# Passages of the chunk scans: first inverse a tile sooner, loads spread, triangular products one by one, casts behind the last zi copy

## The chip, the cores and the metric

The kernel runs on one core of one Trainium2 chip. It is one launch on fp32 data: a whole encoder block with attention, a bidirectional RWKV-7 scan, gates, a squared-ReLU MLP and a gated input embedding. The metric is the device time of one execution in microseconds (us), lower is better. The engines are TensorE (PE, matmuls; PEld are its weight loads), VectorE (DVE), ScalarE (ACT), GpSimd (POOL) and SyncE (SP, which issues most loads).

## The reference, cut to what matters

```python
# x (1, 1024, 1024); 8 query heads, 2 key heads of 64; 8 RWKV heads of 64
proj = rms_norm(x, norm_mix) @ w_in
attn = windowed_gqa(q, k, v, sink)              # +-128 tokens
rw = rwkv7_time_mix(zr, ...)                    # forward and backward scan
gates = sigmoid(proj[..., O_GATE:])             # two branches of 1024 columns
merged = gates[0] * (attn @ w_up_attn) + gates[1] * (rw @ w_up_rwkv)
x = x + merged @ w_out
x = x + square(relu(rms_norm(x, norm_ffn) @ w_ff1)) @ w_ff2
x = x + (p @ w_ple) * sigmoid(rms_norm(x, norm_ple) @ w_ple_gate)

def step(state, inp):                           # the scan, one token
    sa = einsum('dbhij,dbhj->dbhi', state, a_t)
    state = state * w_t + sa * b_t + v_t * k_t
    y = einsum('dbhij,dbhj->dbhi', state, r_t)
```

The change touches the middle of this: attention, the scan, the gates and the lift of the attention by `w_up_attn`.

## The kernel before, in words

**Dense products.** Each fp32 operand is split into a high part (`split`, line 200: a cast on ACT to a shorter matmul type) and the rest (line 201: a subtraction on DVE). A product is three matmuls of parts (hi·hi, lo·hi, hi·lo). Weights arrive as `wst` (or `wust` for `w_up_attn`) and become `whi`/`wlo` (`wuhi`/`wulo`).

**Stages.** First the norm, the projection and the preparation of the RWKV operands, which go to DRAM as `ra_d`, `bk_d`, `v_d`. Then attention in eight tiles `n` of 128 queries. Each makes masked scores `smk` on DVE, transposes them (`pT`), multiplies with the values (`po`) and stores to `at_d`. The gates of the first 512 tokens (half 0) fill PE beside it at the lowest priority: `gates`, 16 products `gmm` over weights `wst`, a tanh `gth` on ACT, a store to `g_d`. `GQ` lists those gates whose weights are loaded by POOL's queue and not by SP's.

**The scan** runs in chunks of 64 tokens, 16 steps `s`, both directions at once, in blocks of four steps. A block needs the inverse of a triangular matrix per chunk and head. Its parts are: the triangular products `lps` of loads `la` and `lb` (`low_products`: per chunk 16 matmuls into two PSUM buffers, evicted by a pair of ACT copies `lt`); four ACT copies `Lc`; a transpose `Lp` and 31 steps of `tmp` and `Z` on DVE; two transposes `Zn` and `Zt`; and `inverse_off`, which makes `Q` and `zi` by small matmuls `qps` with copies (DVE four, ACT four, lines 881 and 882). The first block's products and inverse stand inside the attention, after the tiles that `LOW_AT` and `INV_AT` name. Those of the next blocks stand inside the steps 0, 4 and 8 (`aside(i)`, which calls `low`, and `inverse_steps`, whose DVE steps `inverse_turn` deals out), and `end_inverse` closes them at the end of each fourth step.

**One step** is, in program order: the carried part `wy`, the sum of `W`, the first products `gps` two steps ahead (evicted by DVE as `gm`, line 1187), `gap(0)`, `aside(0)`, `gap(1)`, `u_part` (`ups`, copied by ACT to `UV`; next `wa`, copied to `W`), the second products, `gap(2)`, `gap(3)`, `aside(1)`, `s_part` (`sps`, needs `UV`), `y_part`, `aside(2)`, `gap(4)`, in steps 0, 4 and 8 `aside(3)`, then `gap(5)`, `operands` (`tmps`), and two more gaps. A `gap` is a run of dense matmuls: the gates of half 1, and when these are done the lift of the attention (`uaps`, in `beside`, from `wuhi` and `aTh`). `gps`, `lps`, `qps` and `tmps` share two PSUM buffers.

**What sets the order.** Inside the scan PE's matmuls (`mmo`) and the DVE work marked `turn` stay in program order. Everything else (ACT's casts and copies, DVE's `wlo`, all loads) is placed by a static scheduler. Each engine then works through its list in order, and each DMA queue likewise. `after(x, y)` puts `x` behind `y`.

Of the kernel before, what the change touches and what calls it, by code (L numbers as in the profile page):

```python
# [55 lines left out]
GATT = 0  # L56
GQ = ((0, 1), (0, 2), (1, 0), (1, 1), (1, 2), (1, 3), (1, 4))
LOADS_AT = 6
# [10 lines left out]

LOW_AT = (2, 3)  # L70
INV_AT = 4
GN_EPS = 64e-5
# [75 lines left out]
def block_kernel(ctx: ExitStack, tc: tile.TileContext, I: dict, out: bass.AP):  # L148
# [46 lines left out]

    on_pool = [None]

    def split(hi, lo, src, lo_eng=None, pin=False, behind=None):

        a = nc.scalar.copy(hi, src)  # L200
        b = (lo_eng or nc.vector).tensor_tensor(out=lo, in0=src, in1=hi.bitcast(F32), op=ALU.subtract)  # L201
        for x_, y_ in zip((a, b), behind or ()):
            after(x_, y_)
        if lo_eng is nc.gpsimd:
            on_pool[0] = b
        if pin:
            tc.keep_in_program_order(a)
            tc.keep_in_program_order(b)
        return a, b
# [116 lines left out]
    def gates(h, ms=range(2 * KT), mm=nc.tensor.matmul, lo_of=lambda m: nc.gpsimd):  # L326

        for m in ms:
# [5 lines left out]
            nc.scalar.activation(out=th, in_=ps, func=AF.Tanh, scale=0.5)  # L334
            nc.sync.dma_start(g_d[m, :, 512 * h:512 * h + 512], th)
            yield
# [519 lines left out]
    def inverse_off(pl, ps_of, lt, zz, zi, mm, between):  # L856
# [23 lines left out]
        for k in range(2):  # L880
            nc.scalar.copy(zi[g[0], k::2, 32:64], qss[0][g[2 * k]])
            nc.scalar.copy(zi[g[3], k::2, 0:32], qss[1][g[3 - 2 * k]])

# [117 lines left out]
    sR, sU, sC, sRB = (ExitStack() for _ in range(4))  # L1001
    epi = {}
    def beside():
        def load_at(h):
            for k in range(NP):
                nc.sync.dma_start(epi["at"][k], at_d[:, k, 512 * h:512 * h + 512])

        def load_wu(pl, m):
            st = pl.tile([P, NP, P], F32, name="wust", tag="wu_st", bufs=2)
            nc.sync.dma_start(st, I["w_up_attn"][m])  # L1010
            return st

        yield from gates(1, range(GATT, LOADS_AT), mmo, lo_of=lambda m: nc.vector)
        load_at(0)
        sts = [load_wu(B, m) for m in range(2)]
        yield from gates(1, range(LOADS_AT, 2 * KT), mmo, lo_of=lambda m: nc.vector)
# [15 lines left out]
        def weights(m, st=None):  # L1032
            hi = UA.tile([P, NP, P], F32R, name="wuhi", tag="wu_hi", bufs=3)
            lo = UA.tile([P, NP, P], F32R, name="wulo", tag="wu_lo", bufs=3)
            split(hi, lo, load_wu(UA, m) if st is None else st)
            return hi, lo

        def part(k):
            split(aTh[:, k, :], aTl[:, k, :], epi["at"][k])

# [41 lines left out]
    def epilogue(e):  # L1082
# [17 lines left out]
        def parts2(p, src):  # L1100

            hi, lo = (r.rearrange("q p (a t) -> q p a t", a=2)[:, p] for r in (rwh, rwl))
            split(hi, lo, src)
            return hi, lo
# [231 lines left out]
    def begin_low(b):  # L1336
        lows[b] = low_products(BI, B, 3, ps_gps, b, mmo)
        next(lows[b])
# [10 lines left out]
    load_v(0)  # L1349
    begin_low(1)  # L1350
    for hf in range(2):
# [3 lines left out]
    fill(FILL0)  # L1355
    was = []

    def second_step():
# [13 lines left out]
    for s in range(NCH):  # L1372
# [4 lines left out]
        def gap(i):  # L1377

            fill(FILL[s % NB if s // NB < 3 else 1][i] if more else FILLEND)
# [17 lines left out]
        if nxt:  # L1397
            load_v(s + 1)
        gap(0)
        aside(0)  # L1400
        inverse_turn(TURNS[s % NB][0])
        gap(1)
        W = u_part(s, W)
        if more:
# [3 lines left out]
        gap(3)  # L1408
        aside(1)
        if nxt:  # L1410
            s_part(s)
        y_part(s)
        aside(2)
        gap(4)
        if s % NB == 0 and s // NB < 3:
            aside(3)
            inv[0] = inverse_steps(s // NB + 1)
# [610 lines left out]
```

## Time and profile before

| | |
|---|---|
| time, median of 3 runs | 1656.66 us (1656.21 to 1661.19) |
| the profiled execution | 1657.06 us, span 1655.2 us |
| PE busy | 1598.1 us (97%) |
| DVE / ACT / POOL busy | 1138.6 / 839.3 / 89.6 us |
| DMA | 269.23 MB, mean 163 GB/s |

A timeline row has the start, the duration, the engine, the line, output<-inputs, the shape and a count of instructions; in brackets stand the idle time of the engine just before and what ended it ("issue" is a wait for nothing that the profile shows). The attention runs here up to about 443 us after the span's start, the scan from about 450 to 800. In a table of stretches the fourth number from the end of a row is POOL's busy time with its count, the last three are the granted clock of PE, the DMA share and GB/s.

### The profile page before, as it was taken

The page shows a single profiled execution, that of the slowest core. Times are in us where ns is not written, and L with a number is a line of the kernel's source. Part 1 is how long each engine was busy: PE and PEld are TensorE (multiplying, and loading weights), DVE is VectorE, ACT ScalarE, POOL GpSimd, SP SyncE. Part 2 cuts the span into 40 slices and gives each one's busy share as a digit, 9 for nine tenths or more (in the row PEclk, how much of TensorE's full clock was granted, in tenths as well). Part 3 has the DMA queues.
Part 4 walks back from the last instruction along what each step waited for, and adds up shares of the span by engine and source line. Part 5 has one row for each costly group of instructions (what it writes and reads, how often), then busy time and mean ns, then how long its engine had stood idle before and what let it go on. Part 6 is the DMA issues. An engine that isn't in the chain of part 4 may idle for free.

```text
span 1655.2 us, 31169 instructions
## 1 busy us (share of the span) xinstructions
PE 1598.1 (97%) x12280; PEld 1295.4 (78%) x12280; DVE 1138.6 (69%) x2071; ACT 839.3 (51%) x1533; POOL 89.6 (5%) x111
## 2 busy tenths in 40 slices
PE   7999999999989999799999999999999999999998
PEld 6987777767668777676788778888888888888887
DVE  6648998477939678777826876766658877675332
ACT  5557888378553554555304554444445445444221
POOL 3440000210010000000000000000000000000000
PEclk9999999999999999899999999999999999999999
DMA  6362555855476644458722264444459855564010
GB/s 227 84 151 89 172 175 174 260 160 164 142 222 176 184 140 149 136 186 268 246 80 111 79 195 147 140 148 158 157 185 336 272 189 179 167 199 146 32 42 38
DMA packets 199938, 269.23 MB, mean 163 GB/s; under 512 B 47728, under 2 KB 103920, under 8 KB 199792
## 3 DMA queue, kind: packets, MB, share of 16 engines
q1 hardware_dynamic: 188736, 250.47, 47.5%
q0 software_dynamic: 10912, 16.26, 3.5%
q8 instruction: 96, 1.57, 0.4%
q10 hardware_dynamic: 144, 0.52, 0.1%
q14 instruction: 50, 0.41, 0.1%
HBM read 186.45 MB, written 80.74 MB: 161 GB/s over the span
## 4 chain that ended last, share of the span: by engine, by line
PE 72%; DMA 10%; DVE 7%; ACT 6%; issue 3%; POOL 1%; SPq 0%; ACTq 0%; DVEq 0%; POOLq 0%
PE ff1ps L1657 16%; PE ff2ps L1909 13%; PE gmm L226 5%; DMA wst<-in_w_col_dram 3%; PE mm L244 2%; PE mm L245 2%; PE mm L246 2%; PE plps L236 2%; PE plps L234 2%; PE plps L232 2%; PE gps L226 1%; PE mmo L245 1%; PE mmo L246 1%; PE wy L226 1%; PE mmo L244 1%
## 5 line engine op out<-in xcount | busy, mean ns | idle before, releaser
L1909 PE MATMUL ff2ps<-tl,sh 128*128 128x512 f32 x448 | 174.5, 390 | 0.2 <-DVE tl L201 0.2
L1909 PE MATMUL ff2ps<-th,sl 128*128 128x512 f32 x448 | 174.4, 389 | 0.0
L1909 PE MATMUL ff2ps<-th,sh 128*128 128x512 f32 x448 | 174.0, 389 | 0.0
L200 ACT CAST sh<-sst 128x512 fp32r<-128x512 f32 x109 | 67.8, 622 | 105.7 <-PE ff2ps L1909 50.8
L201 DVE TENSOR_TENSOR sl<-sst,sh 128x512 fp32r<-128x512 f32 x109 | 75.2, 690 | 47.6 <-ACT sh L200 47.2
L1657 PE MATMUL ff1ps<-mh,w1h 128*128 128x512 f32 x256 | 100.3, 392 | 2.0 <-ACT w1h L200 2.0
L200 ACT CAST whi<-wst 128x512 fp32r<-128x512 f32 x100 | 60.3, 618 | 78.7 <-DMA wst<-in_w_col_dram 39.3
L1657 PE MATMUL ff1ps<-ml,w1h 128*128 128x512 f32 x256 | 99.9, 390 | 0.0
L1657 PE MATMUL ff1ps<-mh,w1l 128*128 128x512 f32 x256 | 99.7, 390 | 0.0
L1909 PEld LDWEIGHTS ff2ps<-tl,sh 128*128 128x128 f32 x448 | 84.1, 188 | 18.4 <-DVE tl L201 0.8
L1909 PEld LDWEIGHTS ff2ps<-th,sh 128*128 128x128 f32 x448 | 84.0, 188 | 17.7 <-ACT th L200 0.3
L1909 PEld LDWEIGHTS ff2ps<-th,sl 128*128 128x128 f32 x448 | 84.1, 188 | 17.4
L200 ACT CAST w1h<-w1st 128x512 fp32r<-128x512 f32 x48 | 28.4, 620 | 106.7 <-DMA w1st<-in_w_ff_dram 66.5
L201 DVE TENSOR_TENSOR wlo<-wst,whi 128x512 fp32r<-128x512 f32 x88 | 58.9, 686 | 20.6 <-ACT whi L200 18.6
L185 POOL TENSOR_TENSOR rstd<-ms,neghalf 128x1 f32<-128x1 f32 x24 | 14.8, 615 | 1016.4 <-PE ff2ps L1909 573.1
L201 DVE TENSOR_TENSOR w1l<-w1st,w1h 128x512 fp32r<-128x512 f32 x48 | 31.8, 688 | 49.8 <-ACT w1h L200 49.8
L1657 PEld LDWEIGHTS ff1ps<-mh,w1h 128*128 128x128 f32 x256 | 48.0, 188 | 13.0 <-ACT w1h L200 2.9
L1657 PEld LDWEIGHTS ff1ps<-mh,w1l 128*128 128x128 f32 x256 | 48.1, 188 | 11.1 <-DVE w1l L201 1.0
L1657 PEld LDWEIGHTS ff1ps<-ml,w1h 128*128 128x128 f32 x256 | 48.1, 188 | 10.0
L232 PE MATMUL gmm<-hh,whi 128*128 128x512 f32 x128 | 52.2, 408 | 3.1 <-ACT whi L200 2.5
L1187 DVE TENSOR_TENSOR gm<-gps,gmask 128x384 f32<-128x384 f32 x64 | 32.6, 550 | 31.4 <-PE gps L226 31.2
L226 PE MATMUL gmm<-hl,whi 128*128 128x512 f32 x128 | 52.8, 413 | 1.0 <-issue 1.0
(406 smaller groups left out, 4503.8 us busy)
## 6 DMA issues: line engine op xcount, KB each, us to landing
tst<-in_w_ff_dram SPq DMA_DIRECT2D x80, 256.0 KB, 4.1
wst<-in_w_col_dram SPq DMA_DIRECT2D x78, 256.0 KB, 3.8
w1st<-in_w_ff_dram SPq DMA_DIRECT2D x32, 512.0 KB, 4.9
hid_S<-h SPq DMA_DIRECT2D x64, 256.0 KB, 2.1
sst<-hid_S SPq DMA_DIRECT2D x64, 256.0 KB, 3.4
hid_A<-h SPq DMA_DIRECT2D x48, 256.0 KB, 2.0
sst<-hid_A SPq DMA_DIRECT2D x45, 256.0 KB, 3.8
ra_d<-ra SPq DMA_DIRECT2D x8, 1024.0 KB, 6.1
```

Source lines behind the costliest of these rows:

```text
L200: a = nc.scalar.copy(hi, src)
L201: b = (lo_eng or nc.vector).tensor_tensor(out=lo, in0=src, in1=hi.bitcast(F32), op=ALU.subtract)
L226: tc.keep_in_program_order(nc.tensor.matmul(*a, **kw))
L232: mm(ps, ah, bh, start=(i == 0), stop=False)
L234: mm(ps, ah, bl, start=False, stop=False)
L236: mm(ps, al, bh, start=False, stop=(i == n - 1))
L244: nc.tensor.matmul(ps, ah, bh, start=(i == 0), stop=False)
L245: nc.tensor.matmul(ps, ah, bl, start=False, stop=False)
L246: nc.tensor.matmul(ps, al, bh, start=False, stop=(i == n - 1))
L1187: turn(nc.vector.tensor_tensor(out=gm[hf][:, s % NB, e].rearrange("p (a b) t -> p a b t", b=2), in0=pss[e][:, 0:6].rearrange("p (a b) t -> ...
L1657: nc.tensor.matmul(ps, x_[:, k, :], y_[:, k, :], start=start and k + i == 0, stop=k == 3 and i == 2, skip_group_check=True)
L1909: nc.tensor.matmul(banks[bs][i], x_[:, isl], y_, start=fresh and p + j == 0, stop=p == NPR - 1 and j == 2, skip_group_check=True)
```

## The change

It has six parts.

1. `LOW_AT` goes from (2, 3) to (1, 2) and `INV_AT` from 4 to 3: the first block's triangular products and its inverse stand one attention tile earlier.
2. `GQ` gains (0, 3): the weights of that gate are loaded by POOL's queue.
3. `begin_low(1)`, which issues the first loads `la` and `lb` of the second block, is called behind `operands(0)`.
4. The loads of `at_d` and of the first two `wust` are held behind the last gate store issued ahead of them (`epi["stored"]`).
5. In the steps 0, 4 and 8 the second triangular product stands between `gap(1)` and `u_part`, the third where the second was, and the fourth behind `y_part`, ahead of `gap(4)`. Before, the third and fourth stood around `gap(4)`.
6. The casts of `wuhi`, `aTh` and of the epilogue's `rwh` get `behind=(epi["zi"], None)`: ACT does them behind the last `zi` copy that has been recorded when they are written.

```diff
-GQ = ((0, 1), (0, 2), (1, 0), (1, 1), (1, 2), (1, 3), (1, 4))
+GQ = ((0, 1), (0, 2), (0, 3), (1, 0), (1, 1), (1, 2), (1, 3), (1, 4))
...
-LOW_AT = (2, 3)
-INV_AT = 4
+LOW_AT = (1, 2)
+INV_AT = 3
...
     def split(hi, lo, src, lo_eng=None, pin=False, behind=None):
...
         for x_, y_ in zip((a, b), behind or ()):
-            after(x_, y_)
+            if y_:
+                after(x_, y_)
...
-            nc.sync.dma_start(g_d[m, :, 512 * h:512 * h + 512], th)
+            epi["stored"] = nc.sync.dma_start(g_d[m, :, 512 * h:512 * h + 512], th)
...
-            nc.scalar.copy(zi[g[3], k::2, 0:32], qss[1][g[3 - 2 * k]])
+            epi["zi"] = nc.scalar.copy(zi[g[3], k::2, 0:32], qss[1][g[3 - 2 * k]])
...
-        def load_at(h):
+        def load_at(h, behind=None):
             for k in range(NP):
-                nc.sync.dma_start(epi["at"][k], at_d[:, k, 512 * h:512 * h + 512])
-
-        def load_wu(pl, m):
+                a = nc.sync.dma_start(epi["at"][k], at_d[:, k, 512 * h:512 * h + 512])
+                if behind:
+                    after(a, behind)
+
+        def load_wu(pl, m, behind=None):
             st = pl.tile([P, NP, P], F32, name="wust", tag="wu_st", bufs=2)
-            nc.sync.dma_start(st, I["w_up_attn"][m])
+            a = nc.sync.dma_start(st, I["w_up_attn"][m])
+            if behind:
+                after(a, behind)
             return st
...
-        load_at(0)
-        sts = [load_wu(B, m) for m in range(2)]
+        load_at(0, epi["stored"])
+        sts = [load_wu(B, m, epi["stored"]) for m in range(2)]
...
-            split(hi, lo, load_wu(UA, m) if st is None else st)
+            split(hi, lo, load_wu(UA, m) if st is None else st, behind=(epi["zi"], None))
...
-            split(aTh[:, k, :], aTl[:, k, :], epi["at"][k])
+            split(aTh[:, k, :], aTl[:, k, :], epi["at"][k], behind=(epi["zi"], None))
...
-            split(hi, lo, src)
+            split(hi, lo, src, behind=(epi["zi"], None))
...
     load_v(0)
-    begin_low(1)
     for hf in range(2):
         products(0, hf)
         fill(FILL0)
     operands(0)
     fill(FILL0)
     was = []
+    begin_low(1)
...
+        first = s % NB == 0 and s // NB < 3
         gap(0)
         aside(0)
         inverse_turn(TURNS[s % NB][0])
         gap(1)
+        if first:
+            aside(1)
         W = u_part(s, W)
...
-        aside(1)
+        aside(2 if first else 1)
         if nxt:
             s_part(s)
         y_part(s)
-        aside(2)
+        aside(3 if first else 2)
         gap(4)
-        if s % NB == 0 and s // NB < 3:
-            aside(3)
+        if first:
             inv[0] = inverse_steps(s // NB + 1)
```

A diff row tells little of the lists that come out. Here they are at three places. The first is DVE between the first inverse's end and the first products of the scan (`gm` is the eviction of `gps`, `wlo` belongs to the gates, `zi` are the four DVE copies). Before:

```order
L842 TENSOR_TENSOR Z<-Z,tmp 128x31
L849 STREAM_TRANSPOSE Zn<-Z 128x32x32
L850 STREAM_TRANSPOSE Zt<-Z 128x32x32
L871 COPY zi<-Zn 32x32x32
L1187 TENSOR_TENSOR gm_4576<-gps,gmask 128x384 x2
L871 COPY zi<-Zt 32x32x32 x2
L871 COPY zi<-Zn 32x32x32
L1187 TENSOR_TENSOR gm_4577<-gps,gmask 128x384 x2
L201 TENSOR_TENSOR wlo<-wst,whi 128x512 x2
```

and with the change:

```order
L844 TENSOR_TENSOR Z<-Z,tmp 128x31
L851 STREAM_TRANSPOSE Zn<-Z 128x32x32
L202 TENSOR_TENSOR wlo<-wst,whi 128x512 x2
L873 COPY zi<-Zn 32x32x32 x2
L852 STREAM_TRANSPOSE Zt<-Z 128x32x32
L873 COPY zi<-Zt 32x32x32 x2
L202 TENSOR_TENSOR wlo<-wst,whi 128x512 x2
L1192 TENSOR_TENSOR gm_4576<-gps,gmask 128x384 x2
L1192 TENSOR_TENSOR gm_4577<-gps,gmask 128x384 x2
```

Three `zi` copies and two pairs of `wlo` moved ahead of the first `gm`.

The second is ACT in step 4 (`lt` and `Lc` belong to the triangular products, `UV` and `W` to `u_part`, `whi` and `gth` to the gates, `tm` to `operands`). Before:

```order
L821 COPY lt<-lps 128x4x64 x2
L1304 COPY Lc<-lt 32x256 x4
L1256 COPY UV<-ups 64x512 x2
L1235 COPY W<-wa 128x512
L200 CAST whi<-wst 128x512 x2
L821 COPY lt<-lps 128x4x64 x2
L1304 COPY Lc<-lt 32x256 x4
L1284 COPY y<-wy_6132 128x2x2x64
```

and with the change:

```order
L823 COPY lt<-lps 128x4x64 x2
L1309 COPY Lc<-lt 32x256 x4
L823 COPY lt<-lps 128x4x64 x2
L1309 COPY Lc<-lt 32x256 x4
L1261 COPY UV<-ups 64x512 x2
L1240 COPY W<-wa 128x512
L201 CAST whi<-wst 128x512 x2
L823 COPY lt<-lps 128x4x64 x2
```

The second round of `lt` and `Lc` moved ahead of `UV` and `W`.

The third is ACT at the last closing of an inverse (end of step 11; `rwh` are casts for the epilogue, `wuhi` and `aTh` for the lift of the attention). Before:

```order
L868 COPY Q<-qps 32x16x32 x4
L334 ACTIVATE gth<-gmm 128x512
L200 CAST rwh_8667<-y 128x512 x4
L881 COPY zi<-qps 32x16x32
L882 COPY zi<-qps 32x16x32
L200 CAST wuhi<-wust 128x512
L200 CAST aTh<-gm_4576 128x512 x2
L200 CAST aTh<-gm_4577 128x512 x2
L200 CAST wuhi<-wust 128x512
L881 COPY zi<-qps 32x16x32
L882 COPY zi<-qps 32x16x32
```

and with the change:

```order
L870 COPY Q<-qps 32x16x32 x4
L336 ACTIVATE gth<-gmm 128x512
L883 COPY zi<-qps 32x16x32
L884 COPY zi<-qps 32x16x32
L883 COPY zi<-qps 32x16x32
L201 CAST wuhi<-wust 128x512
L201 CAST aTh<-gm_4576 128x512 x2
L201 CAST aTh<-gm_4577 128x512 x2
L201 CAST wuhi<-wust 128x512
L884 COPY zi<-qps 32x16x32
L201 CAST rwh_8667<-y 128x512 x3
```

The four `rwh` casts moved behind the last `zi` copy; two `wuhi` and four `aTh` still stand ahead of it.

More of the change, by code (lines that the diff above doesn't have):

```diff
@@ L196, in block_kernel @@
     on_pool = [None]
+    epi = {}
     def split(hi, lo, src, lo_eng=None, pin=False, behind=None):
@@ L1001, in block_kernel @@
     sR, sU, sC, sRB = (ExitStack() for _ in range(4))
-    epi = {}
     def beside():
-        def load_at(h):
+        def load_at(h, behind=None):
             for k in range(NP):
-                nc.sync.dma_start(epi["at"][k], at_d[:, k, 512 * h:512 * h + 512])
-        def load_wu(pl, m):
+                a = nc.sync.dma_start(epi["at"][k], at_d[:, k, 512 * h:512 * h + 512])
+                if behind:
+                    after(a, behind)
+        def load_wu(pl, m, behind=None):
             st = pl.tile([P, NP, P], F32, name="wust", tag="wu_st", bufs=2)
-            nc.sync.dma_start(st, I["w_up_attn"][m])
+            a = nc.sync.dma_start(st, I["w_up_attn"][m])
+            if behind:
+                after(a, behind)
             return st
         yield from gates(1, range(GATT, LOADS_AT), mmo, lo_of=lambda m: nc.vector)
-        load_at(0)
-        sts = [load_wu(B, m) for m in range(2)]
+        load_at(0, epi["stored"])
+        sts = [load_wu(B, m, epi["stored"]) for m in range(2)]
         yield from gates(1, range(LOADS_AT, 2 * KT), mmo, lo_of=lambda m: nc.vector)
```

## The prediction

> **What bounds the kernel now.** I read the page first, then the gaps of TensorE (PE) in the timeline, then a table of stretches for the granted clock, then the rows of VectorE (DVE) and ScalarE (ACT) around each gap.
>
> ```profile
> span 1655.2 us, 31169 instructions
> PE 1598.1 (97%) x12280; PEld 1295.4 (78%) x12280; DVE 1138.6 (69%) x2071; ACT 839.3 (51%) x1533; POOL 89.6 (5%) x111
> PE 72%; DMA 10%; DVE 7%; ACT 6%; issue 3%; POOL 1%; SPq 0%; ACTq 0%; DVEq 0%; POOLq 0%
> ```
>
> PE is busy for 97% of the span and carries 72% of the chain that ended last. The change adds no matmul and takes none away, so it can only win where PE stands idle or runs at half clock. The whole of PE's idle time is 1655.2 − 1598.1 = 57.1 us. These are its gaps in the stretch that the change touches (start, duration, work, then the idle time ahead and what ended it):
>
> ```profile
> 454.91 2.01 PE L226 MATMUL gps<-rac,bkc 64*64 64x128 f32 x32 [2.97 <-DVE gm L1187]
> ...
> 466.78 0.62 PE L226 MATMUL wa<-UV,gm 64*64 64x64 f32 x15 [2.00 <-issue]
> ...
> 478.24 0.39 PE L226 MATMUL gmm<-hl,whi 128*128 128x512 f32 x1 [1.01 <-issue]
> ...
> 492.30 1.10 PE L1204 MATMUL tmps<-ident,bkc 128*128 128x128 f32 x5 [0.81 <-ACT lt L821]
> ...
> 545.09 1.01 PE L226 MATMUL gps<-rac,bkc 64*64 64x128 f32 x32 [0.94 <-PE wy L226]
> ...
> 559.15 1.09 PE L1204 MATMUL tmps<-ident,bkc 128*128 128x128 f32 x8 [0.80 <-ACT lt L821]
> ...
> 676.70 0.79 PE L226 MATMUL wy<-rac,Sc 64*64 64x64 f32 x25 [1.34 <-issue]
> 681.39 2.14 PE L226 MATMUL gps<-rac,bkc 64*64 64x128 f32 x32 [3.06 <-ACT zi L881]
> ```
>
> Each part of the change aims at one of these: the first `gm` eviction (2.97), the wait after it (2.00), the triangular products in each fourth step (0.81, 0.80), and the last `zi` copies (3.06). Beside the gaps stands the clock. The next rows are stretches of 3.41 us (and three longer ones): length, then busy time and instructions of PE, weight loads, DVE, ACT and POOL, then granted clock, DMA share and GB/s.
>
> ```profile
> 451.63:455.04 3.41, 0.44 (x4) 0.13 (x4) 3.35 (x5) 0.21 (x2) 0.00 (x0) 1.00 1.14 276
> 455.04:458.45 3.41, 3.41 (x36) 2.75 (x36) 3.35 (x7) 1.11 (x2) 0.00 (x0) 0.50 1.27 214
> 460.00:480.00 20.00, 15.48 (x446) 11.52 (x445) 4.36 (x8) 7.44 (x14) 1.47 (x3) 1.00 0.77 237
> ...
> 489.18:492.59 3.41, 2.13 (x38) 1.33 (x38) 1.29 (x2) 3.31 (x11) 2.19 (x4) 1.00 0.91 221
> 492.59:496.00 3.41, 3.41 (x24) 2.56 (x26) 1.37 (x1) 3.04 (x7) 0.00 (x0) 0.50 0.98 333
> ...
> 680.32:683.74 3.42, 2.35 (x33) 1.99 (x34) 3.24 (x7) 2.19 (x4) 0.00 (x0) 0.50 0.89 282
> 404.00:454.30 50.30, 47.27 (x271) 33.42 (x267) 47.43 (x151) 31.76 (x86) 2.69 (x5) 1.00 0.42 133
> ```
>
> After the 2.97 us gap PE runs 3.41 us at clock 0.50, after which the clock is 1.00 again. Such a passage does half of its work and so costs 3.41 / 2 = 1.7 us. The gap of 2.00 us at 464.78 is followed by none (460 to 480 has 1.00 throughout).
>
> **Part 1: the first inverse one attention tile sooner (LOW_AT, INV_AT).** It neither adds nor removes work; it moves the first block's products and its 31 DVE steps. Here is DVE ahead of the first `gm`, and PE's gate products beside it:
>
> ```profile
> 439.86 0.42 DVE L965 COPY pT<-pt 128x256 f32<-128x256 f32 x1
> ...
> 449.65 2.15 DVE L849 STREAM_TRANSPOSE Zn<-Z 128x1024 f32<-128x1024 f32 x1
> 451.67 1.89 DVE L850 STREAM_TRANSPOSE Zt<-Z 128x1024 f32<-128x1024 f32 x1
> 453.58 0.68 DVE L871 COPY zi<-Zn 32x1024 f32<-32x1024 f32 x1
> 454.30 1.02 DVE L1187 TENSOR_TENSOR gm<-gps,gmask 128x384 f32<-128x384 f32 x2
> ...
> 458.28 1.28 DVE L201 TENSOR_TENSOR wlo<-wst,whi 128x512 fp32r<-128x512 f32 x2
> ```
>
> The first `gm` starts 454.30 − 440.28 = 14.0 us after the last transposed tile of the attention (439.86 + 0.42 = 440.28, the common zero below). The second `gps` product needs its buffer and waits for it. With the change the chain starts one tile sooner: two stores of `at_d` stand at
>
> ```profile
> 419.31 0.53 SPq L974 DMA_DIRECT2D at_d<-at  x1
> 432.87 0.52 SPq L974 DMA_DIRECT2D at_d<-at  x1
> ```
>
> that is 13.56 us apart. But DVE then has three more things to do between the chain's start and the first `gm`. One is an attention tile, which in these groups (busy us, mean ns) is
>
> ```profile
> L943 DVE CUSTOM_DVE_ANT_0 smk<-sc,band 128x256 f32<-128x256 f32 (+1 forms) x8 | 3.5, 451 | 0.2
> L965 DVE COPY pT<-pt 128x384 f32<-128x384 f32 (+1 forms) x5 | 2.5, 527 | 0.2
> L960 DVE TENSOR_SCALAR smk<-smk,es 128x384 f32<-128x384 f32 (+1 forms) x4 | 1.4, 382 | 0.0
> ```
>
> with small ones of about 1.6 beside it: 9.0. The others are, by the order of the changed kernel, four `wlo` (two pairs of 1.28, 2.55) and three `zi` copies (3 × 0.68 = 2.05) that stood behind the first `gm`. That is 13.6 more work for 13.56 us more time. What gains is DVE's idle time: 50.30 − 47.43 = 2.87 us of the stretch 404 to 454 in which it waited, and which the earlier start lets it use. I take 2.2 of it, so the first `gm` starts at +11.8 and its first half is done at +12.4. PE arrives sooner too: the order shows 25 gate matmuls in place of 30 between the attention's last product and the first `gps`, each 0.235 us start to start, so PE wants the second `gps` not at 451.94 − 440.28 = +11.66 but at +10.45. The wait is then 12.4 − 10.45 = 1.95 instead of 2.97, worth 1.0. A wait of 2.00 stands in the quoted rows without half clock, so the 1.7 us of the passage go too: **−2.7**. Bounds: −4.7 (no wait: 2.97 + 1.7), and +0.1, because DVE takes its work in order and the second pair of `wlo` now stands ahead of `gm`. That pair needs its weights, which come on the POOL queue while the DMA share is 1.14 to 1.27: if they land late, `gm` is late, and the stall is as before. The value is nearer the middle because the wait only has to fall under about 2 us.
>
> The Trainium skill ("TensorE: Matmul & The Clock Gate", section "What's actually happening") says that the clock falls to half after an idle window of some 3.4 us, in windows of 3413 ns that run free. The trace agrees on the length of a passage (3.41) and on the window at 451.63, which is nearly idle (0.44 busy). It does not agree at 492.59, where the window before was busy for 2.13.
>
> **Part 2: loads spread.** Half of these eight loads (issues of one line, their ns, first and last start) and two `wust` loads, 1.5 MB in all, move on SP's queue:
>
> ```profile
> L1006 SPq DMA_DIRECT2D gm<-at_d x8: 382/428/659, 472.8 to 681.4; - x8
> ```
>
> from 472.8 to behind the store of gate 5's results, which SP issues near 540. There they stand ahead of two `rac` and two weight loads that have a step to arrive in. They lie under matmuls in both places: the issue wait near the old place is 1.01 (478.24), near the new one 0.94 (545.09, without the burst), so I take 0, with +1.0 if the burst brings a wait to the new place and leaves none saved at the old one. Opening the second block's products moves behind `operands(0)`; its first two pairs of loads keep their place in SP's order, the third now stands behind a gate store. That thins the traffic around 464, where PE waits 2.00 for "issue", twice the other issue waits (1.01, 0.94, 1.34). I take it down to theirs: **−1.0** (0 to −2.0). The gate (0, 3) loads through POOL, ahead of nothing that waits there: 0 (±0.7, half a passage of half clock either way).
>
> The Trainium skill ("Runtime: NRT & Kernel Launch", section "Instruction fetch mechanics") holds that the fetching of instructions is hidden behind their issue. By it these waits are not fetches that traffic delays, and this term is 0, which makes the sum 1651.5 by that rule. No row here says what the wait is.
>
> **Part 3: triangular products one by one.** In steps 0, 4 and 8 four products `lps` are made, each evicted by ACT: a pair of `lt` copies, then four `Lc` copies of it. Before, the third and fourth came together behind `y_part`. ACT in step 4, and the one row that differs in step 0:
>
> ```profile
> 485.50 1.14 ACT L200 CAST whi<-wst 128x512 fp32r<-128x512 f32 x2 [1.63 <-PE gmm L226]
> ...
> 547.90 0.65 ACT L821 COPY lt<-lps 128x256 f32<-128x256 f32 x2 [4.10 <-PE lps L226]
> 548.58 1.65 ACT L1304 COPY Lc<-lt 32x256 f32<-32x256 f32 x4
> 550.23 1.17 ACT L1256 COPY UV<-ups 64x512 f32<-64x512 f32 x2
> ...
> 552.35 1.14 ACT L200 CAST whi<-wst 128x512 fp32r<-128x512 f32 x2 [0.33 <-PE gmm L226]
> ...
> 558.72 0.65 ACT L821 COPY lt<-lps 128x256 f32<-128x256 f32 x2
> 559.39 2.06 ACT L1304 COPY Lc<-lt 32x256 f32<-32x256 f32 x5
> ```
>
> From 547.90 ACT is full up to the `tmps` on PE, which wait (0.80) for the fourth `lt`. The round is thus ACT's: its work is the same, and only its idle time can be won. With a second `lt` and `Lc` (2.30) ready ahead of `UV`, the 1.63 idle of step 0 is filled, and of the 0.33 in step 4 most. By walking ACT's new order with these durations the fourth `lt` ends 1.6 us sooner in step 0 and 0.35 to 0.45 in steps 4 and 8; the last `Lc`, on which DVE's next inverse hangs, 1.35, 0.2 and 0.3 sooner. What PE gains at `tmps` it keeps only so far as the inverse is sooner too, since `qps` wait for that at the block's end. So −1.35 − 0.2 − 0.3 = **−1.85**. Bounds: −4.1 (the whole 1.6 + 0.4 + 0.4, and the passage at 492.59), 0 (all given back at `qps`). New waits lie inside this walk: the second product pair of a step needs the buffers of the second `lps` (about 0.5), `tmps` about 1.1.
>
> **Part 4: casts behind the last `zi` copy.** By the order only the four `rwh` casts move behind; `wuhi` and `aTh` stay ahead of the last copy, since they are written while the name still holds an earlier block's copy.
>
> ```profile
> 674.28 2.17 ACT L200 CAST rwh<-y 128x512 fp32r<-128x512 f32 x4
> ...
> 678.05 2.17 ACT L200 CAST aTh<-gm 128x512 fp32r<-128x512 f32 x4
> ...
> 681.37 0.57 ACT L882 COPY zi<-qps 32x512 f32<-32x512 f32 x1
> ```
>
> Taking out 2.17 does not give 2.17: the `zi` copies need `qps` matmuls on which PE is busy to 676.70 − 1.34 = 675.36. From about 675.2: three copies (1.74), `wuhi` (0.62), `aTh` (2.17), `wuhi` (0.61), last copy (0.57) make 680.9 instead of 681.94: **−1.0**. Bounds 0 (the `aTh` loads come later) and −4.4 (the rest of the 3.06 too, or the half clock there). What the `rwh` are for is the epilogue that starts a step later, so their delay costs nothing; uncovered it would be their own 2.17.
>
> **Sum.** −2.7 − 1.0 − 1.85 − 1.0 = −6.55 against the profiled execution's 1657.06: **1650.5 us**. That execution is 0.4 above the median, so against 1656.66 it is −6.2, or 0.37%. About 0.3% (5.0 us: under 1651.7, over 1661.6) is what can be told from no change.
>
> **Rivals.** (a) *The stall at the first `gm` stays near 3 us* because DVE, in order, waits for the second `wlo` pair, and what ACT's rounds win comes back as waits for `Q` and `Zn`. For it: DMA share over 1 just there. Against: in all of 404 to 454 DVE idles only 2.87. Then the −1.0 of part 2 and some −1.5 of the others remain: about 1654.5. (b) *The change does little of what it says*: casts mostly do not move, products are bound by ACT's total, loads were hidden: −1, about 1656. (c) *The long half clock near 680 breaks.* The quoted row 680.32 is the middle one of three passages at 0.50. By a rule that only an almost idle window brings half clock, the shorter waits there end it: −5.1 less a little, about 1645.5 to 1646. That is the rule cited above; the window at 489.18 speaks against it. (d) *Slower: `UV` behind two rounds of `lt` and `Lc`.* ACT copies `UV` only after the second round, 2.30 us later than now. `s_part` needs it. The cover is the products (32 matmuls, 0.85) and six gate matmuls (1.4) with one `lps` (0.5), 2.75 in all, but PE reaches `u_part` only 0.5 later itself. If ACT takes the second round late because `lps` waits for its buffer, the 2.30 stands bare in three steps (3 × 2.30 = 6.9) and each such wait brings a passage of half clock (3 × 1.7 = 5.1); less the 4.7 of the other parts: about 1664. It decides when `UV` lands after PE's six gate matmuls are done. Against it: by the walk the wait there is about 0.4.
>
> **How the numbers follow.** Forecast 0.50, (a) 0.25, (b) 0.07, (c) 0.08, (d) 0.10. Of the forecast's 0.50 some 0.08 falls within 0.3%, as the sum lies near the bound. Faster: 0.42 + 0.08 = 0.50. Same: 0.25 + 0.07 + 0.08 = 0.40. Slower: 0.10. The range 1643 to 1658 leaves out (d) and a tail beyond (c); its upper end takes in (b) with the +1.0 of the loads.
>
> **What would show it.** The gap ahead of the second `gps` near 450 should be 1.5 to 2.2 with clock 1.00 behind it. The issue wait before `wa` near 465 should be about 1. The fourth `lt` in step 0 should end about 1.6 sooner against the first, with `sps` waiting under 0.6 for `UV`. The gap at the last `gps` should be near 2. A wait of `sps` over 2 us, or a new half clock in steps 4 and 8, proves the forecast wrong; so does a first `gm` that waits for `wlo`.

## The result, and the profile after

| | before | changed |
|---|---|---|
| median of 8 runs | 1657.62 us | 1652.04 us |
| lowest to highest | 1656.21 to 1661.78 | 1648.26 to 1654.46 |
| profiled execution | 1657.06 us | 1652.30 us |

The ratio of the runs is 0.9961, with a 95% interval of 0.9947 to 0.9975. That is faster by 0.39%, or 6.5 us (5.6 us by the medians), where 0.37% (6.2 us) was forecast. The size is right, but the sum was reached by other terms than the prediction's. The page of the changed kernel begins with span and busy time, and its chain that ended last has PE at 73%:

```profile
span 1650.5 us, 31173 instructions
PE 1601.0 (97%) x12280; PEld 1297.2 (79%) x12280; DVE 1136.0 (69%) x2071; ACT 840.0 (51%) x1533; POOL 90.6 (5%) x113
```

PE's idle time fell from 57.1 us to 1650.5 − 1601.0 = 49.5 us, so by 7.6. But PE's busy time, with the same 12280 matmuls, rose by 2.9: it ran longer at half clock (seven passages up to 1640 us, where there were six before). The span fell by the difference, 4.7 us. These are PE's gaps in the timeline of the changed kernel, at the places that the prediction named:

```profile
453.92 0.95 PE L228 MATMUL gps<-rac,bkc 64*64 64x128 f32 x8 [3.03 <-DVE gm L1192]
...
489.88 0.87 PE L1209 MATMUL tmps<-ident,bkc 128*128 128x128 f32 x6 [0.82 <-ACT lt L823]
...
673.37 0.62 PE L228 MATMUL wy<-rac,Sc 64*64 64x64 f32 x26 [0.96 <-issue]
677.70 1.04 PE L228 MATMUL gps<-rac,bkc 64*64 64x128 f32 x28 [2.92 <-ACT zi L884]
```

The wait ahead of the second `gps` is still there, 3.03 after 2.97. The wait of 2.00 at `wa` is gone: no row of that place shows a gap. The `tmps` of step 0 wait as long as before (0.82 after 0.81), but start 2.4 us sooner. Between 450 and 700 us the stretches of 3.41 us at half clock are now these (columns as in the prediction):

```profile
453.01:456.42 3.41, 2.50 (x33) 2.15 (x34) 1.94 (x5) 0.17 (x1) 0.54 (x1) 0.50 1.24 232
456.42:459.83 3.41, 3.41 (x13) 2.92 (x12) 0.41 (x1) 0.69 (x2) 0.00 (x0) 0.50 1.21 258
476.90:480.31 3.41, 3.41 (x39) 2.33 (x37) 0.04 (x1) 1.31 (x4) 0.00 (x0) 0.50 0.27 102
668.04:671.46 3.42, 3.42 (x77) 2.42 (x79) 2.74 (x4) 2.91 (x5) 0.00 (x0) 0.50 0.02 5
678.28:681.70 3.42, 3.42 (x71) 2.56 (x67) 3.42 (x8) 2.09 (x5) 0.00 (x0) 0.50 0.92 287
```

The passage at 492.59 is gone and the three near 680 have become two. The passage behind the first `gps` has become two, and a new one stands at 476.90. So in this part the change has as many passages as before, five.

Where the time went is best read from landmarks of PE that both programs have. `sps` of a step is one. Step 0 has its `sps` here before, then with the change:

```profile
486.02 1.15 PE L226 MATMUL sps<-UV,tm 128*64 128x64 f32 x32
503.85 1.15 PE L226 MATMUL sps<-UV,tm 128*64 128x64 f32 x32
```

```profile
485.11 1.15 PE L228 MATMUL sps<-UV,tm 128*64 128x64 f32 x32
501.06 1.15 PE L228 MATMUL sps<-UV,tm 128*64 128x64 f32 x32
```

The second row is step 1's. From one to the next took 17.83 us before and takes 15.95, so 1.9 less. (The work between the two is not quite the same: one triangular product, 0.6 us of PE, now stands ahead of step 0's `sps` and not behind it. So about 0.6 of the 1.9 belongs in the row above.) Done for all landmarks, this gives the account of the profiled executions (changed minus before, us; negative is sooner):

| up to | difference in position | gained in this stretch |
|---|---|---|
| the first `qps` | +0.1 | +0.1 |
| `sps` of step 0 | −0.9 | −1.0 |
| `sps` of step 1 | −2.8 | −1.9 |
| `sps` of step 3 | −2.3 | +0.5 |
| `sps` of step 5 | −2.8 | −0.5 |
| `sps` of step 7 | −2.8 | 0.0 |
| `sps` of step 9 | −3.3 | −0.5 |
| `sps` of step 11 | −3.3 | 0.0 |
| the first `uaps` | −4.8 | −1.5 |
| the end | −4.7 | +0.1 |

### The profile page after: what moved, and what is told of

Read it like the earlier page. It is cut to its first block, busy times and chain, and to the rows that moved or that the text cites. A ratio compares the mean times of both kernels' runs of the same rounds, so it can differ in the third digit from the quotient of the medians.

```text
span 1650.5 us, 31173 instructions
## 1 busy us (share of the span) xinstructions
PE 1601.0 (97%) x12280; PEld 1297.2 (79%) x12280; DVE 1136.0 (69%) x2071; ACT 840.0 (51%) x1533; POOL 90.6 (5%) x113
## 4 chain that ended last, share of the span: by engine, by line
PE 73%; DVE 9%; DMA 7%; ACT 6%; issue 4%; POOL 1%; SPq 0%; DVEq 0%; POOLq 0%; ACTq 0%
PE ff1ps L1664 16%; PE ff2ps L1916 16%; PE gmm L228 4%; PE plps L238 2%; PE plps L236 2%; PE plps L234 2%; PE mm L246 2%; PE mm L247 2%; PE mm L248 2%; PE mmo L248 1%; PE mmo L246 1%; PE mmo L247 1%; DMA wst<-in_w_col_dram 1%; PE gps L228 1%; PE uaps L228 1%
## 5 line engine op out<-in xcount | busy, mean ns | idle before, releaser
L1916 PEld LDWEIGHTS ff2ps<-th,sh 128*128 128x128 f32 x448 | 84.0, 188 | 17.9 <-ACT th L201 0.3
L1916 PEld LDWEIGHTS ff2ps<-th,sl 128*128 128x128 f32 x448 | 84.1, 188 | 17.4
L228 PE MATMUL gmm<-hh,wlo 128*128 128x512 f32 x128 | 54.2, 423 | 0.0
```

Of the source, the lines that this page charges most:

```text
L228: tc.keep_in_program_order(nc.tensor.matmul(*a, **kw))
L1916: nc.tensor.matmul(banks[bs][i], x_[:, isl], y_, start=fresh and p + j == 0, stop=p == NPR - 1 and j == 2, skip_group_check=True)
```

## The experiments

Seven kernels undo or isolate one part each, c_after is the changed kernel again, and four go on from what the trace showed. All ratios are to the kernel before, run beside them on the same chip; the figure behind is the median.

| run | what it is | ratio, 95% interval | median us |
|---|---|---|---|
| c_after | the changed kernel again | 0.9961 (0.9948 to 0.9973) | 1651.28 |
| x_inv | without the earlier inverse | 0.9975 (0.9964 to 0.9987) | 1652.25 |
| x_aside | without the new places of the products | 0.9996 (0.9983 to 1.0009) | 1655.67 |
| x_step0 | new places in step 0 alone | 0.9972 (0.9957 to 0.9986) | 1653.33 |
| b_aside | before, with the new places alone | 0.9982 (0.9967 to 0.9997) | 1656.09 |
| x_cast | without the held casts | 0.9975 (0.9964 to 0.9985) | 1652.76 |
| x_loads | without the held loads | 0.9963 (0.9949 to 0.9977) | 1651.49 |
| x_gq | without gate (0, 3) on POOL | 0.9965 (0.9952 to 0.9979) | 1652.76 |
| f_wlo | changed, `wlo` behind the first `gm` | 0.9952 (0.9935 to 0.9970) | 1649.01 |
| f_real | changed, casts behind the true last `zi` | 0.9948 (0.9935 to 0.9960) | 1648.64 |
| f_both4 | both, `aTl` on POOL | 0.9934 (0.9921 to 0.9947) | 1646.07 |
| f_three | f_both4, `whi` behind the first closing's `zi` | 0.9914 (0.9894 to 0.9934) | 1643.75 |

One part of the change needs no run. With `begin_low(1)` back at its old place, the lists of all five engines hold the same instructions in the same order as those of the changed kernel. The call was moved, but nothing in the program.

### c_after: the changed kernel again

> The changed kernel again, beside the others on the same chip, as their common base. Expected: ratio to before 0.996 (0.9947 to 0.9975 was measured), the gap ahead of the second gps about 3.0 us with DVE gm as releaser, since the second pair of wlo waits for its weights, and two passages of half clock behind it.

Met in ratio. The profiled execution is another matter: its span is 1646.1 us where the first one had 1650.5, for the same program.

```profile
span 1646.1 us, 31173 instructions
PE 1598.1 (97%) x12280; PEld 1295.4 (79%) x12280; DVE 1136.9 (69%) x2071; ACT 839.9 (51%) x1533; POOL 90.0 (5%) x113
```

PE idles 48.0 us here and 49.5 there, nearly the same; but it is busy for 2.9 us less. So two executions of one program differ by most of what this change is worth, 2.9 us of it in PE's busy time alone, and single profiles are to be compared by stretches, not by spans. The gap ahead of the second `gps` is 3.05, as expected, but the passage behind it is one here, not two:

```profile
454.30:457.71 3.41, 3.41 (x16) 2.92 (x13) 1.02 (x2) 0.44 (x1) 0.00 (x0) 0.50 1.14 264
```

It begins at 454.30, the first one at 453.01: the windows lie otherwise in each execution. (The Trainium skill, "TensorE: Matmul & The Clock Gate", section "What's actually happening", says that the window runs free of the kernel; these two rows agree.)

### x_inv: without the earlier inverse

```diff
-LOW_AT = (1, 2)
-INV_AT = 3
+LOW_AT = (2, 3)
+INV_AT = 4
```

> The changed kernel with LOW_AT and INV_AT back at (2, 3) and 4. Theory: the earlier inverse wins nothing, because the wait for the weights of the second wlo pair took the place of the wait for the inverse; so the time is that of the changed kernel within 1.5 us (ratio to before about 0.996), with a gap of about 3 us ahead of the second gps. Rival: the earlier inverse is worth what its row promised (2.7 us); then this kernel is 2.7 us slower than the changed one, ratio about 0.998.

By the time it is 1.0 us (medians) to 2.3 us (ratios) slower than the changed kernel, and the intervals overlap: unclear between theory and rival. The trace says more. The gap ahead of the second `gps` is 2.78 with the old inverse and 3.05 with the new in c_after, so nothing was won there, as the theory says. What came back is the wait at `wa`. With the old inverse, in x_inv and in b_aside:

```profile
466.43 0.62 PE L228 MATMUL wa<-UV,gm 64*64 64x64 f32 x15 [1.66 <-issue]
```

```profile
467.08 0.62 PE L226 MATMUL wa<-UV,gm 64*64 64x64 f32 x15 [2.01 <-issue]
```

and with the new one, in c_after and in x_loads (below):

```profile
463.65 0.63 PE L228 MATMUL wa<-UV,gm 64*64 64x64 f32 x15 [0.66 <-issue]
```

```profile
463.57 0.63 PE L228 MATMUL wa<-UV,gm 64*64 64x64 f32 x15 [1.04 <-issue]
```

All runs with the earlier inverse have 0 to 1.25 us there, all three with the late one (before among them) 1.66 to 2.01. So the shorter wait comes with this part, where the prediction gave it to the loads. What the wait is, the profile does not say ("issue"); it stays open.

A shorter wait is not yet a gain. Of the eleven traces with the earlier inverse, all but that of f_three run 3.4 to 10.2 us at half clock between 468 and 485; none of the three with the late one does. c_after has two passages there (columns as above):

```profile
471.37:474.78 3.41, 2.66 (x33) 1.72 (x32) 0.32 (x1) 1.58 (x3) 0.00 (x0) 0.50 1.07 318
474.78:478.20 3.42, 3.25 (x37) 2.10 (x36) 0.80 (x2) 0.00 (x0) 0.00 (x0) 0.50 0.19 67
```

From the end of the last transposed tile of the attention to the first `lps` of step 0 the three kernels with the late inverse take 38.5 to 39.5 us. The eight that have the early one and no new edge at `gm` take 37.5 to 40.2, with four or five gate matmuls fewer to do. So up to there the traces show no gain from the earlier inverse: the half clock takes back what the shorter wait gives. Whether the part is worth the 1.0 to 2.3 us of the runs stays open.

### x_aside, x_step0 and b_aside: the triangular products

x_aside puts the products of steps 0, 4 and 8 back, x_step0 those of steps 4 and 8, and b_aside gives the new places to the kernel before.

```diff
# x_aside, against the changed kernel
         gap(1)
-        if first:
-            aside(1)
         W = u_part(s, W)
...
-        aside(2 if first else 1)
+        aside(1)
...
-        aside(3 if first else 2)
+        aside(2)
         gap(4)
         if first:
+            aside(3)
             inv[0] = inverse_steps(s // NB + 1)
# x_step0, against the changed kernel
-        first = s % NB == 0 and s // NB < 3
+        closes = s % NB == 0 and s // NB < 3
+        first = s == 0
...
-        if first:
+        if closes:
+            if not first:
+                aside(3)
             inv[0] = inverse_steps(s // NB + 1)
```

> The changed kernel with the triangular products of steps 0, 4 and 8 back at their old places. Theory: they carry the largest share, 2.4 us by the distance of the steps in the two traces (1.9 in step 0, 0.5 each in steps 4 and 8, 0.5 given back at the first closing); so this kernel is about 2.4 us slower than the changed one, ratio to before about 0.9975, with the fourth lt of step 0 some 1.6 us later and tmps waiting 0.8 in all three steps. Rival: ACT bounds these rounds in any order and the gain came from elsewhere; then within 0.8 us of the changed kernel.

> The changed kernel with the new places of the triangular products in step 0 alone; steps 4 and 8 as before. Theory: the distances between steps in the trace give 1.9 of the gain to step 0 and about 0.5 each to steps 4 and 8, so this kernel is 1.0 us slower than the changed one, ratio to before 0.9967, with tmps waiting 0.8 for lt again in steps 4 and 8. Rival: steps 4 and 8 carry as much as step 0; then 3 us or more slower, ratio 0.998.

> The kernel before with the new places of the triangular products alone. Taking them out of the changed kernel cost 0.35% (ratio 0.9996 against 0.9961). Theory: the parts do not lean on each other, so alone they give most of the whole gain: 3.5 to 5.5 us, ratio 0.9967 to 0.9979. Rival: they pay only beside the earlier inverse and the other parts (the 1.85 of the prediction or less, ratio 0.9985 to 1.0).

This is the part that carries most: without it the kernel is as slow as before (0.9996), and its interval lies clear of the changed kernel's. Alone it gives 0.18%, 3.0 us (1.7 by the medians). Removing it costs more (5.8 us by the ratios, 4.4 by the medians) than adding it gives, but the two intervals, each some ±2 us, do not settle whether the parts lean on each other. x_step0 loses 1.8 us, between its two expectations.

The stretches between `sps` point the same way. From step 0 to step 1 the kernel before takes 17.8 us, x_aside too (486.02 to 503.85, 488.49 to 506.33), and all twelve other traces, which have the new place in step 0, show 15.4 to 16.6. But these stretches differ in more than the wait: with the old places a product of 0.6 us is still to be done in them, and both have a passage of half clock (from 492.6 and 494.8) that none of the twelve has.

A stretch of equal work is that from the first `lps` of a step to its `tmps`. Here it is for step 0 in the kernel before and in b_aside, both without half clock in it:

```profile
479.01 0.27 PE L226 MATMUL lps<-lb,la 64*64 64x64 f32 x1
...
492.30 1.10 PE L1204 MATMUL tmps<-ident,bkc 128*128 128x128 f32 x5 [0.81 <-ACT lt L821]
```

```profile
479.35 0.27 PE L226 MATMUL lps<-lb,la 64*64 64x64 f32 x1
...
490.95 1.09 PE L1204 MATMUL tmps<-ident,bkc 128*128 128x128 f32 x8 [0.36 <-ACT lt L821]
```

It takes 13.3 us before, and 11.6 in b_aside, x_inv and f_three, the three kernels with the new place and no half clock there: 1.7 less. In step 4 it takes 12.0 before, 13.7 in x_aside and 12.9 in x_step0, and 11.6 in seven of the eleven kernels with the new places there (11.7 to 12.6 in the others). In step 8 it takes 11.4 to 11.5 in all three with the old places and 11.0 to 11.1 in all eleven with the new. So up to `tmps` the new places give 1.7, about 0.4 and 0.4 us.

How much of the small gains is kept is less clear. From `sps` of step 7 to that of step 9 the kernels with the new places gain 0.3 to 1.3 on before, but x_step0 and x_aside, with the old ones, gain 0.8 and 0.9 too. So step 0 carries most of it.

The cause is the one that was named: ACT. Here are ACT's rows in step 0, first of x_aside (old places), then of the changed kernel:

```profile
485.71 1.17 ACT L1261 COPY UV<-ups 64x512 f32<-64x512 f32 x2 [0.90 <-PE wa L228]
486.91 0.59 ACT L1240 COPY W<-wa 128x512 f32<-128x512 f32 x1
487.97 1.14 ACT L201 CAST whi<-wst 128x512 fp32r<-128x512 f32 x2 [0.47 <-PE gmm L228]
...
494.34 0.65 ACT L823 COPY lt<-lps 128x256 f32<-128x256 f32 x2
```

```profile
483.71 1.17 ACT L1261 COPY UV<-ups 64x512 f32<-64x512 f32 x2
484.90 0.59 ACT L1240 COPY W<-wa 128x512 f32<-128x512 f32 x1
485.52 1.14 ACT L201 CAST whi<-wst 128x512 fp32r<-128x512 f32 x2
...
489.44 0.67 ACT L823 COPY lt<-lps 128x256 f32<-128x256 f32 x2
```

With the old places ACT stands idle 0.90 and 0.47 and still has a whole round to do between `UV` and the fourth `lt`: 8.6 us. With the new ones it has no gap, and the distance is 5.7. The `UV` copies end at 484.88 and `sps` starts at 485.11 without a wait, so the slower rival of the prediction had no ground: `UV` was covered.

### x_cast: without the held casts

```diff
-            split(hi, lo, src, behind=(epi["zi"], None))
+            split(hi, lo, src)
```

and the same for `wuhi` and `aTh`.

> The changed kernel with no cast held behind a zi copy. Theory: the last zi copy ends 1.0 to 1.8 us later against the last qps, and the kernel is 1 to 1.8 us slower than the changed one, ratio to before 0.9967 to 0.9972; the gap ahead of the last gps grows from 2.9 to 3.1 and the four rwh casts stand ahead of the zi copies again. Rival: the shift seen there came from the clock alone (shorter half-clock passages); then the same time as the changed kernel within 0.5 us.

It is 1.5 us (medians) to 2.3 us (ratios) slower, with overlapping intervals. From `sps` of step 11 to the first `uaps` the kernel before takes 20.4 us. The changed kernel gains 1.5 and c_after 1.1; x_cast and b_aside, which cast `rwh` ahead, gain 0.1 and 0.0. ACT's own rows say the same. This is the last `zi` copy of the changed kernel, whose step 11 has its `sps` at 659.79:

```profile
677.07 0.58 ACT L884 COPY zi<-qps 32x512 f32<-32x512 f32 x1
```

It ends 17.9 us behind that `sps`; in all eight kernels with the casts held as in the change it is 17.4 to 17.9, and 18.7 to 18.8 in the three without (before, b_aside, x_cast). That settles it: the four casts are worth 1.0 to 1.4 us. One expectation failed: the gap ahead of the last `gps` did not grow in x_cast (2.67, with 2.92 and 2.85 in the two traces of the changed kernel), since PE too arrives there at another time.

### x_loads and x_gq: loads

```diff
# x_loads
-        load_at(0, epi["stored"])
-        sts = [load_wu(B, m, epi["stored"]) for m in range(2)]
+        load_at(0)
+        sts = [load_wu(B, m) for m in range(2)]
# x_gq
-GQ = ((0, 1), (0, 2), (0, 3), (1, 0), (1, 1), (1, 2), (1, 3), (1, 4))
+GQ = ((0, 1), (0, 2), (1, 0), (1, 1), (1, 2), (1, 3), (1, 4))
```

> The changed kernel with the at_d and first two wust loads not held behind the gate store (they go back to about 473 in SP's list; nothing else moves in any list). Theory: these 1.5 MB cost nothing at either place, since PE's wait near 464, which went away, comes before them; so the time of the changed kernel within 0.7 us, ratio to before about 0.996. Rival: the burst lengthens the issue waits near 475 to 485 (0.8 in the changed kernel, 1.0 twice before); then 1 to 1.5 us slower.

> The changed kernel with the weights of gate (0, 3) back on SP's queue. Theory: nothing waits for that queue there, so the time of the changed kernel within 0.7 us, ratio to before about 0.996; the gap near 304 that waits for whi is 2.5 again where the changed kernel has 1.3 to 2.1. Rival: that gap and the passage of half clock behind it are what this part buys; then 1.5 to 2 us slower, ratio 0.997 to 0.9975.

x_loads is the changed kernel in time: holding 1.5 MB of loads back had no effect that the runs show. x_gq loses 0.7 us by the ratios, which cannot be told from nothing, but its trace shows a step. The gap near 304, ahead of a gate product that waits for its weights, is in x_gq and in x_loads:

```profile
306.74 0.79 PE L234 MATMUL gmm<-hh,whi 128*128 128x512 f32 x1 [2.40 <-ACT whi L201]
```

```profile
305.26 0.50 PE L234 MATMUL gmm<-hh,whi 128*128 128x512 f32 x1 [1.46 <-ACT whi L201]
```

Without (0, 3) on POOL it is 2.40, and 2.38 in b_aside and 2.47 before; with it, 0.7 to 2.1 in the other runs. The matmul of 0.79 instead of 0.50 runs at half clock. A passage of half clock stands there in all three traces without that load on POOL and in two of the eleven with it. So the rival has something for it, though the runs do not show its 1.5 to 2 us.

### f_wlo: the second wlo pair behind the first gm

```diff
             hi, lo = load_w(PW, "w", w_col(c0), P, parts=2, lo_eng=lo_of(m), q=nc.gpsimd if (h, m) in GQ else None,
+                            behind=(None, epi["gm"]) if (h, m) == (1, 1) else None)
```

(`load_w` hands `behind` to `split`; `epi["gm"]` is the last recorded `gm` eviction.) The trace of the changed kernel gave the reason to try it. DVE and ACT ahead of the first `gm`:

```profile
439.90 0.42 DVE L967 COPY pT<-pt 128x256 f32<-128x256 f32 x1
...
451.20 0.69 DVE L202 TENSOR_TENSOR wlo<-wst,whi 128x512 fp32r<-128x512 f32 x1 [0.60 <-ACT whi L201]
452.71 0.69 DVE L202 TENSOR_TENSOR wlo<-wst,whi 128x512 fp32r<-128x512 f32 x1 [0.81 <-ACT whi L201]
453.32 1.01 DVE L1192 TENSOR_TENSOR gm<-gps,gmask 128x384 f32<-128x384 f32 x2
```

```profile
450.55 0.62 ACT L201 CAST whi<-wst 128x512 fp32r<-128x512 f32 x1 [6.52 <-DMA wst<-in_w_col_dram]
...
452.06 0.62 ACT L201 CAST whi<-wst 128x512 fp32r<-128x512 f32 x1 [0.89 <-DMA wst<-in_w_col_dram]
```

The weights land at 450.5 and 452.0, ACT casts them, DVE subtracts, and only then `gm`.

> The changed kernel with one edge more: the wlo of gate 1 of half 1 are held behind the first products' gm evictions on DVE. Theory: the 3.0 us gap ahead of the second gps is the wait of that wlo pair for its weights, so it falls to about 0.4 to 1.0, and the two half-clock passages behind it (6.8 us at half clock, part of it idle anyway) go with it: 4 to 6 us faster than the changed kernel, ratio to before 0.9925 to 0.9940. Rival: the wait moves to the gate product that needs these wlo, or the gap was the zi copies' all along; then under 1 us faster.

The gap fell to 0.36, and up to the first `qps` the kernel is 5.7 us ahead of before (4.0 to 5.9 ahead of the two traces of the changed kernel), with no half clock there: the theory is shown for this place. But in the time only some 1.5 us (ratios) to 2.3 us (medians) are left of it, with overlapping intervals, because the same thing came up one stage later. PE and ACT of f_wlo at the first closing (the end of the first block's inverse):

```profile
470.23 2.04 PE L228 MATMUL gps<-rac,bkc 64*64 64x128 f32 x30 [3.47 <-ACT zi L884]
```

```profile
467.14 0.62 ACT L201 CAST whi<-wst 128x512 fp32r<-128x512 f32 x1 [4.52 <-DMA wst<-in_w_col_dram]
467.90 0.62 ACT L201 CAST whi<-wst 128x512 fp32r<-128x512 f32 x1 [0.15 <-DMA wst<-in_w_col_dram]
468.43 0.57 ACT L884 COPY zi<-qps 32x512 f32<-32x512 f32 x1
```

ACT, in order, stands 4.52 us at a cast of gate 2 whose weights are late, with the `zi` copies behind it, and `gps` waits for those. Two passages of half clock follow (468.4 to 475.3).

### f_real and f_both4: casts behind the true last zi

In f_real the casts written during the last closing are collected and tied to that closing's own last copy. f_both4 is f_wlo and f_real together, with the four `aTl` on POOL and the second `wuhi` ahead of `aTh`.

```diff
             epi["zi"] = nc.scalar.copy(zi[g[3], k::2, 0:32], qss[1][g[3 - 2 * k]])
+        for a in epi["late"]:
+            after(a, epi["zi"])
```

> The changed kernel with the casts wuhi and aTh that are written inside the last closing held behind that closing's own last zi copy (in the changed kernel the name still holds an earlier block's copy). Theory: the last zi copy ends 3.3 us sooner against the last qps and the 2.9 us gap ahead of the last gps goes, but DVE then does wulo, four aTl and wulo 0.6 us later than now and ahead of the sum of W, so PE waits at ups for W instead: 0.5 to 1.2 us faster than the changed kernel, ratio to before 0.9953 to 0.9958. Rival: the zi copies alone set this place; then 2.5 to 4.2 us faster (gap and the half clock behind it).

> f_wlo's edge together with the held casts, and what stands ahead of the sum of W on DVE taken away: the four aTl are made by POOL and the second wuhi is cast ahead of aTh. Theory: DVE reaches the sum of W about 2.3 us sooner than in the changed kernel, so this closing gives 2.0 us and perhaps its half-clock passage (1.7), beside the 4 to 6 of the wlo edge: 6 to 9 us faster than the changed kernel, ratio to before 0.9905 to 0.9925. Rival: POOL's aTl (1.4 each for this shape before) make uaps wait instead; then no better than f_wlo alone.

f_real is 2.2 us (ratios) faster than the changed kernel, between theory and rival, and the intervals overlap; the trace decides. From `sps` of step 11 to the first `uaps` it gains 3.1 on before instead of 1.5, and the 2.9 us gap is gone. The wait for `W` that the theory feared is not there. f_both4 gains 4.0 in that stretch. Its `uaps` wait for POOL, as its rival said, though only for 0.92:

```profile
672.31 0.50 PE L230 MATMUL uaps<-aTl,wuhi 128*128 128x512 f32 x1 [0.92 <-POOL aTl L204]
```

Its gap at the first closing is 4.06. Its time, 4.5 us (ratios) under the changed kernel, misses the 6 to 9 expected: that gap was not in the expectation, and what it costs the next kernel shows.

### f_three: one edge more

```diff
-                            behind=(None, epi["gm"]) if (h, m) == (1, 1) else None)
+                            behind=(None, epi["gm"]) if (h, m) == (1, 1) else (epi["zi"], None) if (h, m) == (1, 2) else None)
```

> f_both4 with one edge more: the whi casts of gate 2 of half 1 held on ACT behind the first closing's last zi copy. Theory: the 3.5 to 4.1 us gap that came up at the first closing once the wlo wait was gone is ACT, in order, standing at a whi cast whose weights land late, ahead of the zi copies; with the edge the gap falls to 0.7 to 1.2 and part of the 6.8 us at half clock behind it goes: 2.5 to 4.5 us faster than f_both4 (median 1646.1), so 1641.6 to 1643.6, ratio to before 0.9907 to 0.9920. Rival: the late weights are wanted by gate 2's products right behind, so the wait only moves there; then within 1 us of f_both4.

The gap is 0.90, with no half clock behind it (none up to 661):

```profile
469.15 1.48 PE L230 MATMUL gps<-rac,bkc 64*64 64x128 f32 x31 [0.90 <-ACT zi L888]
```

It is 2.3 us (medians) to 3.3 us (ratios) faster than f_both4; these two intervals overlap, but the gap and the half clock are gone as the theory says. With a ratio of 0.9914 (0.9894 to 0.9934) it beats both kernels: 14 us under before, 8 us under the change.

## Why the prediction was right

The forecast of 1650.5 us missed the median by 1.5 us. The terms in their order:

- **Part 1 (−2.7): wrong, it gave nothing at its place.** The walks were good. PE wanted the second `gps` at +10.6, where +10.45 was forecast. The first `gm` was put at +11.8 after the last transposed tile, which ends here at 439.90 + 0.42 = 440.32; it started at 453.32, so at +13.0, of which 0.60 + 0.81 = 1.41 are waits for late weights. Without these it is +11.6. What failed is the step from walk to wait: the second `wlo` pair was taken as ready. Its late landing was there as the lower bound (+0.1) and as rival (a), with 0.25, and it is what happened. f_wlo shows it by taking it away. The second passage of half clock behind that wait (in the first execution) and those between 468 and 485 were not foreseen.
- **Part 2 (−1.0): wrong in cause, and the gain is not shown.** The wait of 2.00 at `wa` did fall to between 0 and 1.25. But x_loads keeps the fall without the held loads, and x_inv loses it without the earlier inverse. The step "that thins the traffic around 464" is refuted, and moving `begin_low(1)` changed no list at all. Nor did the shorter wait count in full, as the half clock behind it shows. The 0 for gate (0, 3) was mis-sized as an effect on its gap, which shrank from about 2.4 to 0.7 to 2.1 us; as an effect on the time it cannot be told from 0.
- **Part 3 (−1.85): right in mechanism, too small by the runs.** The walk had the fourth `lt` end 1.6 us sooner in step 0 and 0.35 to 0.45 in steps 4 and 8; `tmps` comes 1.7, about 0.4 and 0.4 sooner. The runs give 3.0 (alone) and 5.8 us (removed), each some ±2 us. The passage at 492.59, which stood only in the bound of −4.1, went as well, but it did not cost the 1.7 us of the prediction's rule: from `tmps` of step 0 to the next `sps` it took 11.55 us with the passage before and 11.18 without it in the changed kernel, 0.4 less.
- **Part 4 (−1.0): right.** 1.0 to 1.4 us, and only the four `rwh` casts moved, as the order had shown. The gap there did not fall to 2 (2.92 and 2.85), as PE arrives sooner too.

Of the rivals, (a) held for its first half; its second half, that the rounds' gain is given back at the closings, is not seen: the second and third closing (`zi` copies from 539 and 605) lie in the stretches up to `sps` of steps 5 and 9, which gain 0.5 each. The 0.5 us (1.1 in c_after) lost between steps 1 and 3 lies at no closing, against what the expectation of x_aside says; the other kernels lose 0.0 to 1.1 there, and why stays open. (b) fell with x_aside. (c) did not come: the half clock near 680 became shorter but stayed, and its number of passages differs between executions. (d) fell: `UV` lands in time.

So the total was in part luck: −3.7 of the −6.55 stood for gains that the traces do not show, and other gains made up for them. Those that the traces place (1.7, 0.4 and 0.4 in the rounds, 1.0 to 1.4 at the casts) come to 3.5 to 3.9 of the 5.6 to 6.5 us measured. The other 2 to 3 us have no shown place; the earlier inverse, by the runs of x_inv, and gate (0, 3) are candidates. A right total is no proof of the working.

## What to carry to other kernels

When an edit lets work start sooner, list what stands ahead of the next needed instruction in the new order of that engine, and ask of each item when its DMA lands: an engine that works in order stops at the first late one, however little it matters. Here a few such edges, which put casts and subtractions that could wait behind evictions that could not, were worth as much as the whole change. Compare stretches between landmarks over several kernels, not the spans of two profiles, when the clock scatters the total by as much as the effect.

## What the runs showed of the hardware that was not expected

- Two profiled executions of the same program differed by 4.4 us in span (1650.5 and 1646.1), with PE's idle time within 1.5 us. The other 2.9 us are busy time of the same 12280 matmuls: up to 1640 us one has seven passages of half clock and the other five. The passages of 3.41 us behind the first `gps` began at 453.01 in one and at 454.30 in the other.
- The same place has one passage of half clock or two behind gaps of the same length (3.05 in c_after, 3.03 in the first execution).
- How busy PE was in the 3.41 us ahead does not tell whether half clock follows. In c_after it was busy for 2.66 us from 467.96 to 471.37, with no gap over 0.6, and half clock followed; in b_aside it was busy for 1.64 us from 463.43 to 466.84, and none did. Short gaps are no safeguard: 0.36 in f_wlo and 0.90 in f_three brought none at their places, 0.72 and 0.77 in the changed kernel stood ahead of the passage at 476.90.
